# Chunk-band attention beside a gated convolution: taps between the gate's products, end transposes ahead of the second exponential, low parts last in the value products

## The chip, the core and the metric

The kernel runs on one core of one Trainium2 chip. Its engines are TensorE (PE in the profile, with PEld for its weight loads), VectorE (DVE), ScalarE (ACT), GpSimd (POOL) and SyncE (SP, which here only issues DMAs). Each takes its own instructions in the order in which the program gives them, and waits for the others through semaphores. The metric is the device time of one execution in microseconds (us); the kernel before takes 1465.99 us, the median of 3 runs between 1465.03 and 1468.26.

## What is computed

One layer of a streaming encoder, over 2048 prompt frames and 32 frames of a running stream (2080 tokens, width 1024, fp32):

```python
xn = rmsnorm(x, norm_in)
h, bg, cg, zc, q, k, v, za = project_in(xn, w_in)     # 8 x 512 columns
u = cg * h
yc = bg * short_conv(u_ext, conv_w, S) * silu(zc)     # three causal taps along time
ya = band_attention(q, k, v, ...) * silu(za)          # own chunk of 64 and 8 before, 8 heads
x = x + merge_out(yc, ya, norm_conv, norm_att, w_out)
x = per_layer_embed(x, p, ple_norm, w_ple_gate, w_ple_proj)
```

The three taps: `out = w[0] * u_ext[:, 0:length]`, then `out + w[t] * u_ext[:, t:t + length]` for t = 1, 2. The newest keys, values and convolution rows are returned as well.

## The kernel before

Every matrix product is split: a matrix is held as a high part and a low part (what rounding took off), and a product is three products on TensorE, high by high, high by low, low by high. Columns of the projection are worked off in "slots" of 2 x 128 channels, tokens in five chunks of 256, 384, 512, 512 and 416.

The program has four stages. Keys, queries, values and the attention gate come first (to about 400 us of the profiled execution). Then follow the convolution's slots in three passes over the chunks: (0, 1), (2, 3), (4). The first pass runs alone. Beside the second and the third the attention is woven in: `dense()` yields after every three products of `conv` (one contraction slice `k`), and between two yields the main loop takes one "piece" of `attention()` whenever the convolution is ahead of its share. The last stage is the output projection, the embedding gate and the final norm.

`conv(u, banks)` treats one slot. Odd slots are (h, C): they write U = C * h. Even ones are (B, z): block `j == 0` is B, block `j == 1` is z, 24 products each, accumulated in a PSUM bank. Behind the last product of B come the taps: ACT writes T1 (L1097), DVE adds two taps to it (L1099), and DVE multiplies the bank by it (T2, L1102). Behind z come the gate (L1105 to L1107) and the store. All of it is emitted at one place, so on DVE's queue it is one row of instructions.

The attention goes through 68 steps (head pair, 256 queries, head), each with two score blocks `a` of 128 queries by up to 640 keys. One step `n` is six pieces:

- scores of block 0 on PE (L546), and on DVE the bias and the maximum (L558), which reads the scores' two banks; there is only one pair of such banks, so the next scores wait for this maximum
- value products of step n-2 on PE (L650 to L664), and on ACT the exponential of block 0 (L566)
- first transposes of step n-1 (L618), evacuated twice: the high part by ACT (L592), the low part by DVE (L593); then reciprocal (L572, DVE) and normalisation (L578, POOL) of block 0
- scores and maximum of block 1
- second transposes of step n-1, then the exponential of block 1
- the end transposes of step n-1 (L627, L628), then reciprocal and normalisation of block 1

`emit_av` multiplies the values with both parts of the transposed weights (`hi`, `lo`). Middle key tiles go 256 columns at a time (L664); the two end tiles are taken in three products of 64 rows and 128 columns each (L662), ahead of the last middle product.

Of the kernel before, what the change touches and what calls it, by code (L numbers as in the profile page):

```python
# [63 lines left out]
def hybrid_encoder_kernel(  # L64
# [574 lines left out]
    def emit_av(n):  # L639
        p, m, h = steps[n]  # L640
        hi, lo = PT
        p_min = max(0, 4 - 2 * m)
        w = 256 if m < 8 else 2 * S

        heads = [(h, 0)] if m < 8 else [(0, 0), (1, 256 + w)]
        if m == 8:
            for g, _ in heads:
                for k in (1, 2, 3, 0, 4):
                    nk = 256 if k else 128
                    pe.matmul(PS[:, PS_AV, 256 * g:256 * g + nk],  # L650
                              V[:, (16 + k) % RING, g * 128:(g + 1) * 128],
                              hi[:, slot_of[k], 0:nk], start=(k == 1), stop=(k == 4))
        else:
            v = lambda k: V[:, (2 * m - 4 + k) % RING, h * 128:(h + 1) * 128]
            both = [(k, t) for k in range(max(p_min, 1), 5) for t in (hi, lo)]
            for i, (k, t) in enumerate(both):
                if i == len(both) - 1:

                    for k1 in [0, 5] if p_min == 0 else [5]:
                        cs = slice(0, 128) if k1 == 0 else slice(128, 256)  # L660
                        for part, t1 in ((0, hi), (0, lo), (1, hi)):
                            pe.matmul(PS[0:HD, PS_AV, cs], v(k1)[:, part * HD:(part + 1) * HD],  # L662
                                      t1[:, slot_of[k1], cs], start=False, stop=False)
                pe.matmul(PS[:, PS_AV, 0:256], v(k), t[:, slot_of[k], :], start=(i == 0),  # L664
                          stop=(i == len(both) - 1))
        if h == 0:
            ytiles[p, m] = y_r()
        y = ytiles[p, m]
        own = lambda g: slice(64 * g, 64 * g + 64)
        for g, c in heads:  # L670
            act.activation(OFF[own(g), 0:w], PS[own(1 - g), PS_AV, c:c + w], AF.Copy)  # L671
        for g, c in heads:
            dve.tensor_tensor(y[own(g), 0:w], PS[own(g), PS_AV, c:c + w], OFF[own(g), 0:w],
                              ALU.add)
        if h == 1 or m == 8:
            t0, t1 = m * 256, min(m * 256 + 256, TT)
            yt = y[:, 0:t1 - t0]
            if m == 8:
                pool.tensor_tensor(yt, yt, y[:, S:2 * S], ALU.add)
            pool.tensor_tensor(yt, yt, Z[(9 * p + m) % 2][:, 0:t1 - t0], ALU.mult)  # L680
            sp.dma_start(yd[DC + p * 128:DC + (p + 1) * 128, t0:t1], yt)

    def attention():
# [3 lines left out]
        for n in range(N + 2):  # L687
# [24 lines left out]
            if n < N and steps[n][1] == 8:  # L712
                load_bias8(steps[n][0] + 1)
            yield
            if tr:
                tr.pop(0)()
            emit_exp(n, 1)
            yield
            if tr:
                tr.pop(0)()  # L720
            emit_recip(n, 1)
            emit_norm(n, 1)
            if n - 1 in first_of:
# [338 lines left out]
    dve.tensor_scalar(cwh, cT[:, 24:36], 0.5, None, ALU.mult)  # L1062
    dve.memset(carry, 0.0)

    def conv(u, banks):

        kind, cc = slots[NP1 + u % 8][0]
# [8 lines left out]
        for c in chunks:  # L1076
# [3 lines left out]
            for j in range(2):  # L1080
                ps = PS[:, banks(), 0:n]
                js = slice(j * 128, (j + 1) * 128)
                for k in range(KT):
                    for i, (a, b) in enumerate(((wh, Xh), (wh, Xl), (wl, Xh))):
                        pe.matmul(ps, a[:, k, js], b[c][:, k, :], start=(k == i == 0),  # L1085
                                  stop=(k == KT - 1 and i == 2))
                    if k < KT - 1:
                        yield n
                if kind == "h" and j == 0:
                    act.activation(HS[:, :n], ps, AF.Copy)  # L1090
                elif kind == "h":
                    for o, w, x in segs:
                        dve.tensor_tensor(U[:, x:x + w], ps[:, o:o + w], HS[:, o:o + w], ALU.mult)
                elif j == 0:
                    cw = lambda t: cwh[:, 4 * t + cc:4 * t + cc + 1]
                    for o, w, x in segs:
                        act.activation(T1[:, o:o + w], U[:, x - 2:x - 2 + w], AF.Copy, scale=cw(0))  # L1097
                        for t in (1, 2):
                            dve.scalar_tensor_tensor(  # L1099
                                T1[:, o:o + w], U[:, x - 2 + t:x - 2 + t + w], cw(t),  # L1100
                                T1[:, o:o + w], ALU.mult, ALU.add)
                    dve.tensor_tensor(T2[:, :n], ps, T1[:, :n], ALU.mult)  # L1102
                else:

                    act.activation(SZ[:, :n], ps, AF.Tanh, scale=0.5)  # L1105
                    dve.scalar_tensor_tensor(SZ[:, :n], SZ[:, :n], 1.0, ps, ALU.add, ALU.mult)  # L1106
                    pool.tensor_tensor(T2[:, :n], T2[:, :n], SZ[:, :n], ALU.mult)  # L1107
                    sp.dma_start(yd[cc * 128:(cc + 1) * 128, t0:t0 + n], T2[:, :n])
                yield n
# [107 lines left out]
```

## Time and profile before

| | before |
|---|---|
| median of 3 runs | 1465.99 us |
| the profiled execution | 1465.2 us |
| its span, first to last instruction | 1463.2 us |
| granted TensorE clock, mean of the span | 0.992 |
| busy: PE, PEld | 97%, 87% |
| busy: DVE, ACT, POOL | 42%, 37%, 21% |

The profiled execution's own time is 2.0 us longer than its span, and 0.8 us below the median. TensorE is the engine that is nearly always busy. The others have much idle time, and what matters of them is only whether TensorE has to wait for them. A busy share of the whole span hides the stages, so the rows below are read by stretch and as single instructions in order of time.

### The profile page before, as it was taken

What the parts mean: (1) busy time and instruction counts of PE and PEld (TensorE: products, weight loads), DVE (VectorE), ACT (ScalarE), POOL (GpSimd) and SP (SyncE); (2) the same over time, 40 slices, a digit from 0 to 9 for tenths busy, and PEclk for the clock granted to TensorE, in tenths of its full rate; (3) what the DMA queues carried; (4) which work ended last, traced back from release to release, by engine and by line L of the source; (5) the groups of instructions that cost most, each with busy time, mean ns of one, the idle gap of its engine ahead of it and who ended that gap; (6) DMA issues with size and microseconds to landing.
All of it is one profiled execution on the core that took longest, in us unless ns stands there. A gap on an engine that the chain in (4) does not pass through costs nothing.

```text
span 1463.2 us, 22734 instructions
## 1 busy us (share of the span) xinstructions
PE 1426.2 (97%) x8362; PEld 1269.9 (87%) x8362; DVE 609.4 (42%) x1346; ACT 543.5 (37%) x1182; POOL 314.0 (21%) x438
## 2 busy tenths in 40 slices
PE   8999999999999979999999999998999999999997
PEld 8889989999899968888888888997788888888786
DVE  6323233330044326656555566653424333242333
ACT  7434233341233125544544544552122232232323
POOL 3310000000000013323332232331223232233322
PEclk9999999999999999999999999999999999999999
DMA  6536898884277555453555347666932212121100
GB/s 222 196 109 198 294 314 312 292 286 149 79 249 260 213 183 180 159 163 122 170 174 195 126 148 270 251 231 232 363 102 69 72 48 93 48 80 40 60 25 33
DMA packets 176391, 249.10 MB, mean 170 GB/s; under 512 B 19564, under 2 KB 124816, under 8 KB 170136
## 3 DMA queue, kind: packets, MB, share of 16 engines
q1 hardware_dynamic: 169712, 235.83, 47.6%
q10 hardware_dynamic: 6568, 11.82, 2.5%
q8 instruction: 66, 1.08, 0.3%
q14 instruction: 45, 0.37, 0.1%
HBM read 158.23 MB, written 92.50 MB: 171 GB/s over the span
## 4 chain that ended last, share of the span: by engine, by line
PE 86%; DMA 5%; DVE 3%; issue 2%; ACT 2%; SPq 1%; POOL 1%; POOLq 0%; DVEq 0%; ACTq 0%
PE PS L1085 20%; PE PS L279 17%; PE PS L280 16%; PE PS L281 16%; PE PS L546 5%; PE PS L664 3%; PE PS L618 3%; DMA GR<-wd 2%; PE PS L662 1%; PE PS L871 1%; DMA GR<-qs 1%; PE PS L829 1%; PE PS L268 1%; DMA GF<-ext 1%; DVE GF L1099 1%
## 5 line engine op out<-in xcount | busy, mean ns | idle before, releaser
L279 PE MATMUL PS<-GR 128*128 128x512 f32 (+3 forms) x1336 | 476.2, 356 | 2.9 <-DVE GF L1120 1.8
L280 PE MATMUL PS<-GR 128*128 128x512 f32 (+3 forms) x1336 | 471.9, 353 | 1.1 <-DVE GR L271 0.6
L281 PE MATMUL PS<-GR 128*128 128x512 f32 (+3 forms) x1336 | 471.9, 353 | 0.5 <-DVE GR L812 0.5
L1085 PE MATMUL PS<-GR 128*128 128x512 f32 (+3 forms) x1920 | 432.1, 361 | 0.6 <-DMA GR<-wc 0.6
L1085 PEld LDWEIGHTS PS<-GR 128*128 128x128 f32 x1920 | 310.8, 191 | 16.8 <-DMA GR<-wc 0.9
L279 PEld LDWEIGHTS PS<-GR 128*128 128x128 f32 x1336 | 253.2, 190 | 34.2 <-DVE GF L1120 2.1
L281 PEld LDWEIGHTS PS<-GR 128*128 128x128 f32 x1336 | 253.1, 189 | 31.6 <-DVE GR L812 1.0
L280 PEld LDWEIGHTS PS<-GR 128*128 128x128 f32 x1336 | 253.4, 190 | 30.9 <-DMA GR<-wd 1.1
L578 POOL TENSOR_SCALAR GF<-GF,SM 128x640 f32<-128x640 f32 (+3 forms) x132 | 98.5, 746 | 265.7 <-DVE SM L572 195.8
L593 DVE TENSOR_TENSOR GR<-PS,GR 128x256 fp32r<-128x256 f32 (+2 forms) x184 | 103.2, 562 | 98.9 <-ACT GR L592 98.7
L592 ACT ACTIVATE GR<-PS 128x256 fp32r<-128x256 f32 (+2 forms) x184 | 89.8, 489 | 78.4 <-PE PS L618 76.7
L1107 POOL TENSOR_TENSOR GF<-GF 128x512 f32<-128x512 f32 (+3 forms) x20 | 22.4, 1122 | 409.1 <-DVE GF L1106 408.4
L566 ACT ACTIVATE GF<-GF,SM 128x640 f32<-128x640 f32 (+3 forms) x132 | 99.9, 757 | 22.7 <-DVE SM L558 21.4
L558 DVE CUSTOM_DVE_ANT_0 GF<-PS,GF 128x640 f32<-128x640 f32 (+3 forms) x132 | 96.2, 729 | 24.7 <-PE PS L546 20.8
L546 PE MATMUL PS<-GR 128*128 128x320 f32 (+6 forms) x512 | 94.9, 307 | 11.7 <-DMA GR<-qs 7.4
L546 PEld LDWEIGHTS PS<-GR 128*128 128x128 f32 x512 | 81.4, 190 | 20.9 <-issue 7.7
L910 DVE TENSOR_TENSOR GF<-PS,GF 128x512 f32<-128x512 f32 (+2 forms) x35 | 23.6, 675 | 176.3 <-ACT GF L909 176.3
L909 ACT ACTIVATE GF<-PS,SM 128x512 f32<-128x512 f32 (+2 forms) x35 | 23.6, 675 | 163.9 <-PE PS L281 82.7
L664 PE MATMUL PS<-GR 128*128 128x256 f32 x448 | 78.0, 289 | 3.0 <-DVE GR L593 3.0
L195 DVE SCALAR_TENSOR_TENSOR GR<-GF,cT,GR 128x256 fp32r<-128x256 f32 x112 | 45.8, 480 | 73.9 <-ACT GR L194 73.9
L912 POOL TENSOR_TENSOR GF<-GF 128x512 f32<-128x512 f32 (+1 forms) x32 | 41.1, 1285 | 159.7 <-DVE GF L910 141.5
L671 ACT ACTIVATE GF<-PS 64x256 f32<-64x256 f32 (+1 forms) x72 | 26.0, 360 | 130.7 <-PE PS L664 124.2
(139 smaller groups left out, 1344.4 us busy)
## 6 DMA issues: line engine op xcount, KB each, us to landing
GR<-wc SPq DMA_DIRECT2D x32, 1024.0 KB, 7.3
GR<-wd SPq DMA_DIRECT2D x72, 256.0 KB, 6.8
GF<-in_x_prompt_dram SPq DMA_DIRECT2D x32, 512.0 KB, 7.6
wc<-GR SPq DMA_DIRECT2D x16, 1024.0 KB, 7.6
GR<-qs SPq DMA_DIRECT2D x128, 128.0 KB, 3.2
wd<-GF SPq DMA_DIRECT2D x50, 256.0 KB, 6.1
GF<-in_w_in_dram SPq DMA_DIRECT2D x20, 512.0 KB, 6.0
vd<-GF SPq DMA_DIRECT2D x40, 256.0 KB, 5.1
```

Of the source, the lines that this page charges most:

```text
L195: dve.scalar_tensor_tensor(wl[:, k], RAW[:, k], cT[:, k:k + 1], wh[:, k].bitcast(F32), ALU.mult, ALU.subtract)
L279: pe.matmul(out, wh(k), xh(k), start=(k == ks_[0]), stop=False)
L280: pe.matmul(out, wh(k), xl(k), start=False, stop=False)
L281: pe.matmul(out, wl(k), xh(k), start=False, stop=(k == ks_[-1]))
L546: pe.matmul(ps[:, e, c:c + n_], q[h][b][:, qa], K[h][:, r:r + n_], start=(b == 0 and c == 0), stop=(b == 1), skip_group_check=True)
L558: dve.tensor_tensor_reduce(pr.rearrange("p (b c) -> p b c", b=nb), ps, br.rearrange("p (b c) -> p b c", b=nb), 1.0, 3e38, ALU.add, ALU.min ...
L566: act.activation(pr, pr, AF.Exp, bias=mx[rows], scale=-1.0, accum_out=sm[rows])
L578: pool.tensor_scalar(pr, pr, rs[rows], 1.0, ALU.mult, ALU.mult)
L592: act.activation(dst_of(hi), src, AF.Copy)
L593: dve.tensor_tensor(dst_of(lo), src, dst_of(hi).bitcast(F32), ALU.subtract)
L664: pe.matmul(PS[:, PS_AV, 0:256], v(k), t[:, slot_of[k], :], start=(i == 0), stop=(i == len(both) - 1))
L1085: pe.matmul(ps, a[:, k, js], b[c][:, k, :], start=(k == i == 0), stop=(k == KT - 1 and i == 2))
```

## The change

Three pieces of code move, and none is added or taken away.

The taps of `conv` go out of the place behind B's last product. A new function `tap` emits tap 0 (ACT) after the products of slice k = 1 of the block B, tap 1 after k = 3 and tap 2 after k = 5 (both DVE). Only the product T2 stays behind the last product. In `attention` the end transposes and their evacuation move from the sixth piece into the fifth, ahead of the second exponential. In `emit_av` the high parts of all middle tiles are multiplied first and then the low parts, and the ends go high, high, low.

```diff
-            both = [(k, t) for k in range(max(p_min, 1), 5) for t in (hi, lo)]
+            both = [(k, t) for t in (hi, lo) for k in range(max(p_min, 1), 5)]
...
-                        for part, t1 in ((0, hi), (0, lo), (1, hi)):
+                        for part, t1 in ((0, hi), (1, hi), (0, lo)):
...
             yield
-            if tr:
+            while tr:
                 tr.pop(0)()
             emit_exp(n, 1)
             yield
-            if tr:
-                tr.pop(0)()
             emit_recip(n, 1)
             emit_norm(n, 1)
...
+    TAP_AT = (1, 3, 5)
+
+    def tap(t, cc, segs):
+        cw = cwh[:, 4 * t + cc:4 * t + cc + 1]
+        for o, w, x in segs:
+            src = U[:, x - 2 + t:x - 2 + t + w]
+            if t == 0:
+                act.activation(T1[:, o:o + w], src, AF.Copy, scale=cw)
+            else:
+                dve.scalar_tensor_tensor(T1[:, o:o + w], src, cw, T1[:, o:o + w],
+                                         ALU.mult, ALU.add)
...
+                    if kind == "B" and j == 0 and k in TAP_AT:
+                        tap(TAP_AT.index(k), cc, segs)
                     if k < KT - 1:
                         yield n
...
                 elif j == 0:
-                    cw = lambda t: cwh[:, 4 * t + cc:4 * t + cc + 1]
-                    for o, w, x in segs:
-                        act.activation(T1[:, o:o + w], U[:, x - 2:x - 2 + w], AF.Copy, scale=cw(0))
-                        for t in (1, 2):
-                            dve.scalar_tensor_tensor(
-                                T1[:, o:o + w], U[:, x - 2 + t:x - 2 + t + w], cw(t),
-                                T1[:, o:o + w], ALU.mult, ALU.add)
                     dve.tensor_tensor(T2[:, :n], ps, T1[:, :n], ALU.mult)
```

VectorE's queue at the B block of the second pass whose taps run at 657 us of the profiled execution, before (L558 is a maximum, L593 a low part, L572 a reciprocal, L673 the sum of the two value halves):

```order
L558 ISA GF,SM<-PS,GF 128x384
L558 ISA SM 128x1
L673 TENSOR_TENSOR GF<-PS,GF 64x256
L572 RECIPROCAL SM<-SM 128x1
L558 ISA GF,SM<-PS,GF 128x512
L558 ISA SM 128x1
L593 TENSOR_TENSOR GR<-PS,GR 128x256
L1099 SCALAR_TENSOR_TENSOR GF<-GF,cwh 128x512 x2
L1102 TENSOR_TENSOR GF<-PS,GF 128x512
L593 TENSOR_TENSOR GR<-PS,GR 128x128
L572 RECIPROCAL SM<-SM 128x1
```

The same place now (L1073 is a tap, L1108 is T2):

```order
L1073 SCALAR_TENSOR_TENSOR GF<-GF,cwh 128x512
L558 ISA GF,SM<-PS,GF 128x384
L558 ISA SM 128x1
L673 TENSOR_TENSOR GF<-PS,GF 64x256
L1073 SCALAR_TENSOR_TENSOR GF<-GF,cwh 128x512
L572 RECIPROCAL SM<-SM 128x1
L558 ISA GF,SM<-PS,GF 128x512
L558 ISA SM 128x1
L593 TENSOR_TENSOR GR<-PS,GR 128x256
L593 TENSOR_TENSOR GR<-PS,GR 128x128
L1108 TENSOR_TENSOR GF<-PS,GF 128x512
L572 RECIPROCAL SM<-SM 128x1
```

The two taps left the place between the two low parts for places in front of a maximum and in front of a reciprocal, the second low part (the ends') stands directly behind the first, and T2 stands behind both.

The same queue at the B block whose taps run at 587 us, before:

```order
L673 TENSOR_TENSOR GF<-PS,GF 64x256
L593 TENSOR_TENSOR GR<-PS,GR 128x512
L572 RECIPROCAL SM<-SM 128x1
L1099 SCALAR_TENSOR_TENSOR GF<-GF,cwh 128x512 x2
L1102 TENSOR_TENSOR GF<-PS,GF 128x512
L558 ISA GF,SM<-PS,GF 128x640
L558 ISA SM 128x1
L593 TENSOR_TENSOR GR<-PS,GR 128x512
```

And now:

```order
L1073 SCALAR_TENSOR_TENSOR GF<-GF,cwh 128x512
L673 TENSOR_TENSOR GF<-PS,GF 64x256
L593 TENSOR_TENSOR GR<-PS,GR 128x512
L572 RECIPROCAL SM<-SM 128x1
L1108 TENSOR_TENSOR GF<-PS,GF 128x512
L558 ISA GF,SM<-PS,GF 128x640
L558 ISA SM 128x1
L593 TENSOR_TENSOR GR<-PS,GR 128x512
```

In front of the maximum only T2 is left; one tap stands ahead of L673, and the other one a maximum further up.

ScalarE's queue in a step of the second pass without a tap, before (L566 is an exponential, L592 a high part; the last one is that of the ends):

```order
L671 ACTIVATE GF<-PS 64x256
L566 ACTIVATE GF,SM<-GF,SM 128x640
L592 ACTIVATE GR<-PS 128x512 x2
L566 ACTIVATE GF,SM<-GF,SM 128x640
L592 ACTIVATE GR<-PS 128x2x128
```

And now:

```order
L671 ACTIVATE GF<-PS 64x256
L566 ACTIVATE GF,SM<-GF,SM 128x640
L592 ACTIVATE GR<-PS 128x512 x2
L592 ACTIVATE GR<-PS 128x2x128
L566 ACTIVATE GF,SM<-GF,SM 128x640
```

The ends' high part went ahead of the second exponential.

## Rows read from the trace of the kernel before

**Rows 1.** The page's line of busy time, share of the span and instructions of each engine.

```profile
PE 1426.2 (97%) x8362; PEld 1269.9 (87%) x8362; DVE 609.4 (42%) x1346; ACT 543.5 (37%) x1182; POOL 314.0 (21%) x438
```

**Rows 2.** Busy time by stretch: the first pass of the convolution, and the second and third with the attention beside them. Columns: stretch, its length, busy time and instructions of PE, PEld, DVE, ACT and POOL, granted clock of PE, DMA share, GB/s.

```profile
400.00:520.00 120.00, 120.00 (x802) 118.75 (x801) 43.54 (x104) 35.13 (x83) 8.33 (x12) 1.00 0.65 230
520.00:1016.00 496.00, 475.32 (x3076) 425.20 (x3075) 278.89 (x744) 231.55 (x565) 140.86 (x215) 0.99 0.56 187
```

**Rows 3.** The waits view of PE between 580 and 1010 us: who waited, for whom, total us, times, longest.

```profile
PE PS L546 <- DVE SM L558: 4.3, 4, 1.7
PE PS L662 <- DVE GR L593: 4.2, 2, 2.2
PE PS L664 <- DVE GR L593: 3.0, 3, 1.3
PE PS L618 <- POOL GF L578: 0.8, 3, 0.3
```

**Rows 4.** The timeline around the taps at 657 us: start, duration, engine, line, operation, tiles, count, and in brackets the idle time before and what ended it.

```profile
657.10 0.25 ACT L592 ACTIVATE GR<-PS 128x128 fp32r<-128x128 f32 x1
657.23 1.54 DVE L1099 SCALAR_TENSOR_TENSOR GF<-GF,cwh 128x512 f32<-128x512 f32 x2 [1.16 <-ACT GF L1097]
657.61 0.22 PE L662 MATMUL PS<-GR 128*64 128x128 f32 x1
658.86 0.69 DVE L1102 TENSOR_TENSOR GF<-PS,GF 128x512 f32<-128x512 f32 x1
659.47 0.28 DVE L593 TENSOR_TENSOR GR<-PS,GR 128x128 fp32r<-128x128 f32 x1
659.80 0.34 PE L662 MATMUL PS<-GR 128*64 128x128 f32 x2 [1.97 <-DVE GR L593]
```

**Rows 5.** The timeline around the taps at 587 us, same columns.

```profile
587.15 1.94 DVE L1099 SCALAR_TENSOR_TENSOR GF<-GF,cwh 128x512 f32<-128x512 f32 x2
587.43 1.12 POOL L578 TENSOR_SCALAR GF<-GF,SM 128x640 f32<-128x640 f32 x1 [1.13 <-DVE SM L572]
589.29 0.69 DVE L1102 TENSOR_TENSOR GF<-PS,GF 128x512 f32<-128x512 f32 x1 [0.20 <-DVE GF L1099]
589.89 0.81 DVE L558 CUSTOM_DVE_ANT_0 GF<-PS,GF 128x640 f32<-128x640 f32 x1
590.77 0.41 PE L546 MATMUL PS<-GR 128*128 128x320 f32 x1 [1.72 <-DVE SM L558]
```

**Rows 6.** Busy time by stretch, columns as in Rows 2: two short stretches behind the waits at 657 and 774 us, and the three long ones around them.

```profile
661.70:665.10 3.40, 3.40 (x12) 2.72 (x11) 1.19 (x4) 0.28 (x2) 0.89 (x2) 0.50 0.50 161
777.80:781.10 3.30, 3.30 (x11) 2.52 (x10) 0.92 (x3) 1.33 (x4) 1.53 (x3) 0.50 0.14 43
581.70:661.60 79.90, 75.88 (x498) 66.28 (x497) 45.14 (x122) 38.48 (x97) 22.80 (x40) 1.00 0.50 164
665.20:777.70 112.50, 108.94 (x711) 95.10 (x711) 67.84 (x176) 55.75 (x137) 34.07 (x53) 1.00 0.47 152
781.20:1016.00 234.80, 229.52 (x1538) 212.21 (x1537) 133.63 (x353) 109.52 (x263) 66.42 (x98) 1.00 0.62 213
```

**Rows 7.** The taps on DVE between 530 and 1010 us: count, shortest, median and longest duration in ns, first and last start, forms; they belong to 11 B blocks.

```profile
L1099 DVE SCALAR_TENSOR_TENSOR GF<-GF,cwh x28: 239/750/1168, 562.7 to 989.5; 128x512 f32<-128x512 f32 x16, 128x384 f32<-128x384 f32 x6, 128x32 f32<-128x32 f32 x6
```

**Rows 8.** From the groups by line and form between 520 and 1010 us: count, busy us, mean ns of one, idle before.

```profile
L1099 DVE SCALAR_TENSOR_TENSOR GF<-GF,cwh 128x512 f32<-128x512 f32 x16 | 13.3, 832 | 2.3 <-ACT GF L1097 2.1
L1102 DVE TENSOR_TENSOR GF<-PS,GF 128x512 f32<-128x512 f32 x8 | 5.5, 691 | 1.2 <-DVE GF L1099 0.6 <-PE PS L618 0.2
```

**Rows 9.** The timeline of a step without a tap: a maximum, its read-out, and the scores behind it; then the second exponential's read-out, the ends' high part and low part, and the reciprocal.

```profile
603.43 0.82 DVE L558 CUSTOM_DVE_ANT_0 GF<-PS,GF 128x640 f32<-128x640 f32 x1
604.17 0.08 DVE L558 DVE_READ_ACCUMULATOR2_ANT SM<- 128x1 f32 x1
604.31 0.95 PE L546 MATMUL PS<-GR 128*128 128x320 f32 x6
...
605.03 0.18 ACT L566 ACTIVATION_READ_ACCUMULATOR GF<-GF,SM 128x1 f32 x1
605.12 0.36 ACT L592 ACTIVATE GR<-PS 128x256 fp32r<-128x256 f32 x1
605.51 0.42 DVE L593 TENSOR_TENSOR GR<-PS,GR 128x256 fp32r<-128x256 f32 x1 [0.50 <-ACT GR L592]
605.85 0.15 DVE L572 RECIPROCAL SM<-SM 128x1 f32<-128x1 f32 x1
```

**Rows 10.** The timeline around 884 us: a product on POOL, a copy of two columns on DVE, and the scores that waited.

```profile
883.86 1.29 POOL L1107 TENSOR_TENSOR GF<-GF 128x512 f32<-128x512 f32 x1 [0.64 <-DVE SM L572]
883.90 1.28 DVE L1075 COPY GF<-cT 128x2 f32<-128x2 f32 x1
885.57 0.61 PE L546 MATMUL PS<-GR 128*128 128x384 f32 x2 [0.47 <-DVE SM L558]
```

**Rows 11.** The timeline at the end of the first pass, and the first scores of the attention.

```profile
516.46 0.56 DVE L1102 TENSOR_TENSOR GF<-PS,GF 128x384 f32<-128x384 f32 x1 [9.39 <-DMA yd<-GF]
527.97 0.75 PE L546 MATMUL PS<-GR 128*128 128x128 f32 x2 [7.35 <-DMA GR<-qs]
```

**Rows 12.** The timeline of the last B block, where the last stage begins.

```profile
1016.00 1.06 ACT L811 ACTIVATE GR<-GR 128x1024 fp32r<-128x1024 f32 x1 [13.62 <-DMA GR<-yd]
1023.00 0.50 PE L279 MATMUL PS<-GR 128*128 128x512 f32 x1 [1.85 <-DVE GF L1120]
```

## The prediction

> **What bounds the kernel now.** I read the page's busy shares first, then busy time by stretch, then the waits of TensorE, then single instructions around each wait, and last the granted clock behind them. TensorE is busy 97% of the span and every other engine under half [rows 1], so an instruction on another engine costs time only where TensorE waits for it. The stretches show where that can be: in the convolution's first pass, 400 to 520 us, TensorE is busy 120.00 of 120.00 us, and there the taps hold up nothing that counts; in the second and third pass, with the attention beside them, it is busy 475.32 of 496.00 us, which leaves 20.7 us idle [rows 2]. Of these 7.35 us are one wait at 528 us for queries [rows 11]. The rest is mostly in the waits view from 580 to 1010 us: 4.3 us of scores (L546) waiting for a maximum (L558), 4.2 and 3.0 us of value products (L662, L664) waiting for a low part (L593), 0.8 us of transposes waiting for POOL [rows 3].
>
> The single instructions show what these have in common. At 657 us the ends' high part is done at 657.35, and its low part, 0.28 us long, could start. But VectorE's queue holds the two taps (1.54 us) and T2 (0.69 us) in front of it; the low part runs at 659.47, and TensorE has waited 1.97 us for it [rows 4]. At 587 us the same three instructions stand in front of a maximum. It runs at 589.89 instead of about 587.2, and the next scores wait 1.72 us [rows 5]. The reader is to see a queue taken in order: 2.2 to 2.6 us of work that nobody waits for, ahead of 0.3 to 0.9 us for which TensorE waits. I followed the nine rows of waits of rows 3 on DVE to their places: eight stand behind such a bunch; the ninth, 0.47 us, stands behind a copy [rows 10].
>
> **The taps.** The change removes no instruction. 11 B blocks lie in the attention's stretch, with 28 tap instructions on DVE [rows 7], in 22 places (the third pass cuts a tap in two). Before, each block's pair and its T2 were one bunch: 2 x 0.83 + 0.69 = 2.35 us by the means [rows 8]. Now the largest piece is one tap, 0.83 us, or T2. Of the waits this takes away those behind a bunch: 4.3 - 0.47 + 4.2 + 3.0 = 11.0 us [rows 3, 10].
>
> A second term hangs on the first. Behind the waits of about 2 us at 657 and 774 us the granted clock is 0.50, that is 1.2 in place of 2.4 GHz, for 3.4 and 3.3 us; the long stretches around them have 1.00, though the shorter waits lie in them, that of 1.72 us among them [rows 5, 6]. Work done at half the clock takes twice the time, so half of 6.7 us was lost: 3.35 us. Without the two waits I expect no fall there.
>
> Against this stands what a single tap costs at its new place. It is put between the products, and so in front of whatever DVE does there: a maximum, a low part, a reciprocal. The trace does not show a tap there, so I bound it. From below: nothing, since DVE is busy only 278.89 of 496.00 us there [rows 2], and an idle stretch hides a tap. Less than nothing I exclude for this part, since the order of the other instructions is kept. From above: all of it on TensorE at all places, 13.3 us for the 16 long ones [rows 8] and 6 x 0.75 = 4.5 us for the third pass by the median [rows 7], 17.8 us. What decides is the room between a maximum and the scores behind it. It can be thin: in one step the read-out ends at 604.25 and the scores start at 604.31 [rows 9]. But a whole bunch of 2.35 us cost TensorE 11.0 / 8 = 1.4 us on average at eight of the 11 blocks and nothing at three, so that about 1 us and more was covered each time, and a single tap is mostly covered. I take the lower end and add three waits of the size of the thin case at 885.57, 0.47 us each [rows 10]: 1.4 us given back.
>
> Tap 0 moves on ScalarE from behind B to slice 1, where it needs U. In the third pass U is written right before, so ScalarE may stand behind DVE for part of a microsecond, three times, with an exponential behind it. I put this into the 1.4 us. The first pass and the last B block keep their waits. At 516 us T2 waits for the store of the previous T2, and the queries come after that store [rows 11]; neither depends on the taps. At 1016 us the last block's taps stand on ScalarE behind an instruction that waits 13.62 us for a transfer [rows 12], and they still stand behind it.
>
> **The end transposes.** Two transposes a step go one piece earlier on TensorE, which costs it nothing, since the normalised weights that they read are the ones that the first transposes have read already. On ScalarE the second exponential now starts one high part later, 0.36 us. On DVE the reciprocal still comes behind the ends' low part, but that one no longer comes behind the exponential: before, the reciprocal started at 605.85, 0.64 us behind the read-out at 605.21 [rows 9]; now the read-out would end 0.36 us later, at 605.57, and the reciprocal could follow directly. So POOL's normalisation starts some 0.2 us earlier, not later. Bounds: all of TensorE's waits for POOL gone, 0.8 us [rows 3], or three of them longer by 0.36 us, 1.1 us. I take zero. What the move also does is to bring the ends' low part ahead of T2, which helps at 657 us even if the taps alone did not.
>
> **The value products.** Here the wait for a low part moves back by one to three products, of which each is a small part of the waits of 2 us. It works on the same 7.2 us as the taps and can't win them a second time. As cover for the thin cases it is inside the 1.4 us.
>
> **The sum.** 11.0 + 3.35 - 1.4 = 13.0 us. The profiled execution took 1465.2 us, 2.0 us more than its span and 0.8 us less than the median, so 1465.2 - 13.0 + 0.8 gives 1453.0 us.
>
> **The rivals.** First, the waits go, but the clock falls elsewhere as often as before, since other gaps stay: 1465.2 - 11.0 + 1.4 + 0.8 = 1456.4 us. For it speaks that the wait of 7.35 us stays; against it, that from 781 to 1016 us, with two of the three waits on L664 and the one of rows 10 in it, the clock held 1.00 [rows 6].
>
> Second, the taps meet POOL. A copy of two columns took 1.28 us beside a product on POOL of 1.29 us, from start to end [rows 10]. POOL is busy 140.86 of 496.00 us there [rows 2], 28%, so some 6 of 22 taps would meet it; if each held DVE for 1.13 us more where it has no room, 6.8 us would come back: 1459.8 us. Against it speaks that the tap pair beside POOL took 1.94 us [rows 5] where the one without took 1.54 us [rows 4]: 0.4 us more, not 1.1. The Trainium skill, "SBUF — State Buffer", section "Who interferes with whom", holds that VectorE and GpSimd share one pair of ports and that it is an exclusive lock, behind which the loser waits for the whole instruction. The trace agrees for the copy and not for the taps; by the rule taken literally the forecast would be this rival's.
>
> Third, the change does not do what it says: the maximum was late for another reason than the bunch, and the waits come back at other steps. Then the time stays within 0.2% of before, about what a measurement of this kernel can tell from no change, 1466 us. Against it stands that nothing else was in front of the late instructions [rows 4, 5].
>
> Fourth, slower: every single tap lands in front of a maximum whose scores have no room, as at 604.31 [rows 9]. Then 17.8 us come in for the 14.35 us that go, 1465.2 + 3.4 + 0.8 = 1469.4 us. It decides from the point where four in five taps (14.35 of 17.8) are without cover; DVE's idle 44% speaks against that.
>
> **How the numbers follow.** Chances: the forecast 0.62, the first rival 0.15, the second 0.13, the third 0.05, the fourth 0.05. The forecast's own range goes from 1448.5 us (nothing given back, POOL's 0.8 us won, and some 2 us that the modelled ends of the matmuls hide) to 1457 us. The first rival lies inside. About half of the second does if the range ends at 1459 us. That holds 0.62 + 0.15 + 0.06 = 0.83. Faster by over 0.2% (under 1463.1 us): 0.62 + 0.15 + 0.13 = 0.90; same 0.05; slower 0.05.
>
> **What would show it.** In the waits of TensorE between 580 and 1010 us, no row on L593's successor, and 1.5 us or less behind the maximum: the taps' term. Granted clock 1.00 in every stretch from 581 to 1010 us: the clock's term; a 0.50 there with the waits gone speaks for the first rival. Taps of 1.2 us and more beside POOL, with scores waiting behind them, for the second. Waits for POOL's normalisation above 0.8 us would show the end transposes mis-sized. The waits at 528 and 1023 us should stand as they are. The forecast is wrong if maxima wait behind single taps at many steps.

## The result and the profile after

The changed kernel takes 1450.59 us (median of 6 runs, 1448.02 to 1454.36), the one before 1465.51 us (6 runs, 1462.56 to 1468.26). The ratio is 0.990, with a 95% interval of 0.988 to 0.992: about 15 us, or 1.0%, faster. The prediction was 1453.0 us, in a range of 1448.5 to 1459.0 us.

The profiled execution of the kernel after took 1452.0 us with a span of 1450.1 us, 13.1 us shorter than the span before. The page's line of busy time shows the same work as [rows 1]:

```profile
PE 1421.2 (98%) x8362; PEld 1270.3 (88%) x8362; DVE 607.8 (42%) x1346; ACT 542.3 (37%) x1182; POOL 317.4 (22%) x438
```

Busy time by stretch (columns as in [rows 2]): the first pass, the one short stretch at half clock beside the attention, and the rest of the attention's stretch:

```profile
400.00:520.00 120.00, 120.00 (x803) 118.86 (x802) 43.62 (x104) 34.63 (x83) 8.33 (x12) 1.00 0.65 229
524.30:534.60 10.30, 6.24 (x17) 5.12 (x18) 0.89 (x5) 1.10 (x4) 0.37 (x1) 0.50 0.92 311
534.60:1003.00 468.40, 464.52 (x3062) 421.06 (x3060) 276.77 (x740) 230.14 (x562) 142.84 (x214) 1.00 0.56 189
```

The first pass is as it was. To compare the attention's stretch one has to cut both traces at the same work. These two windows hold the same 3078 products of TensorE, up to the first product of the output projection (L279); the first is the kernel before, the second the kernel after:

```profile
520.00:1017.11 497.11, 475.86 (x3078) 425.33 (x3076) 278.90 (x745) 232.66 (x567) 140.86 (x215) 0.99 0.56 187
520.50:1002.56 482.06, 470.94 (x3078) 426.07 (x3077) 277.23 (x745) 231.37 (x567) 143.21 (x215) 0.99 0.57 192
```

So the attention's stretch is 15.05 us shorter, 2 us more than the span. Of that, 0.5 us was lost ahead of 520.50 us and 1.5 us behind 1002.56 us, where TensorE waits 1.8 us for the last stage's weights (1.12, 0.17 and 0.50 us) and the kernel before 0.5 us. Inside the stretch TensorE's idle time went from 497.11 - 475.86 = 21.25 to 482.06 - 470.94 = 11.12 us, which is 10.1 us. The other 4.9 us are busy time, of which the granted clock explains about half, as worked out below.

The waits of TensorE between 520 and 995 us show what went (columns as in [rows 3]; the row of the queries answers to the 7.35 us in [rows 11]):

```profile
PE PS L546 <- DMA GR<-qs: 7.2, 1, 7.2
PE PS L618 <- POOL GF L578: 2.0, 3, 0.7
PE PS L546 <- DVE SM L558: 0.5, 1, 0.5
PE PS L1096 <- DMA GR<-wc: 0.4, 1, 0.4
```

The 7.2 us for low parts are gone, and of the 4.3 us for maxima 0.5 us is left, the wait behind the copy of [rows 10]. POOL's row grew. The timeline at the place of [rows 4], now at 655 us, shows the cause at work:

```profile
654.73 0.56 ACT L592 ACTIVATE GR<-PS 128x256 fp32r<-128x256 f32 x2 [1.08 <-PE PS L618]
...
655.18 0.62 DVE L593 TENSOR_TENSOR GR<-PS,GR 128x256 fp32r<-128x256 f32 x2
...
655.72 0.68 DVE L1108 TENSOR_TENSOR GF<-PS,GF 128x512 f32<-128x512 f32 x1
...
657.14 0.34 PE L662 MATMUL PS<-GR 128*64 128x128 f32 x3
```

Both low parts come straight behind their high parts, and T2 (L1108) stands behind them. The product L662, which had waited 1.97 us, has no bracket: it waits for nothing.

### The profile page after: what moved, and what is told of

Same layout as the page of the kernel before. It is cut to its first block, busy times and chain, and to the rows that moved or that the text cites. A ratio compares the mean times of both kernels' runs of the same rounds, so it can differ in the third digit from the quotient of the medians.

```text
span 1450.1 us, 22728 instructions
## 1 busy us (share of the span) xinstructions
PE 1421.2 (98%) x8362; PEld 1270.3 (88%) x8362; DVE 607.8 (42%) x1346; ACT 542.3 (37%) x1182; POOL 317.4 (22%) x438
## 4 chain that ended last, share of the span: by engine, by line
PE 90%; DMA 4%; issue 2%; DVE 2%; ACT 1%; POOL 1%; SPq 1%; POOLq 0%; ACTq 0%; DVEq 0%
PE PS L1096 22%; PE PS L279 17%; PE PS L280 17%; PE PS L281 17%; PE PS L546 5%; PE PS L664 4%; PE PS L618 3%; PE PS L662 1%; PE PS L869 1%; PE PS L827 1%; PE PS L268 1%; DMA GR<-wd 1%; DMA GF<-ext 1%; DVE GR L209 1%; DMA GR<-qs 0%
## 5 line engine op out<-in xcount | busy, mean ns | idle before, releaser
L279 PE MATMUL PS<-GR 128*128 128x512 f32 (+3 forms) x1336 | 476.4, 357 | 4.2 <-DVE GF L1126 1.7
L279 PEld LDWEIGHTS PS<-GR 128*128 128x128 f32 x1336 | 253.4, 190 | 35.6 <-DVE GF L1126 1.9
L578 POOL TENSOR_SCALAR GF<-GF,SM 128x640 f32<-128x640 f32 (+3 forms) x132 | 99.7, 756 | 243.7 <-DVE SM L572 178.3
L593 DVE TENSOR_TENSOR GR<-PS,GR 128x256 fp32r<-128x256 f32 (+2 forms) x184 | 97.6, 559 | 73.3 <-ACT GR L592 72.9
L1113 POOL TENSOR_TENSOR GF<-GF 128x512 f32<-128x512 f32 (+3 forms) x20 | 22.4, 1121 | 411.4 <-DVE GF L1112 400.6
L592 ACT ACTIVATE GR<-PS 128x256 fp32r<-128x256 f32 (+2 forms) x184 | 83.7, 491 | 75.5 <-PE PS L618 74.8
L558 DVE CUSTOM_DVE_ANT_0 GF<-PS,GF 128x640 f32<-128x640 f32 (+3 forms) x132 | 96.9, 734 | 28.4 <-PE PS L546 24.6
L566 ACT ACTIVATE GF<-GF,SM 128x640 f32<-128x640 f32 (+3 forms) x132 | 100.4, 761 | 16.6 <-DVE SM L558 15.8
```

The lines of the kernel that those rows point to most:

```text
L279: pe.matmul(out, wh(k), xh(k), start=(k == ks_[0]), stop=False)
L558: dve.tensor_tensor_reduce(pr.rearrange("p (b c) -> p b c", b=nb), ps, br.rearrange("p (b c) -> p b c", b=nb), 1.0, 3e38, ALU.add, ALU.min ...
L566: act.activation(pr, pr, AF.Exp, bias=mx[rows], scale=-1.0, accum_out=sm[rows])
L578: pool.tensor_scalar(pr, pr, rs[rows], 1.0, ALU.mult, ALU.mult)
L592: act.activation(dst_of(hi), src, AF.Copy)
L593: dve.tensor_tensor(dst_of(lo), src, dst_of(hi).bitcast(F32), ALU.subtract)
```

## The experiments

Each was timed in five rounds against the kernel before; ratios carry their 95% intervals. Kernels of one job shared a chip and the runs of before: e1 to e4 (before 1465.59 us), e5 to e8 (1466.27), e9 to e11 (1466.14), e12 (1466.09). The theory was that of the prediction: a bunch on DVE's queue is in front of short work for which TensorE waits. The rivals were that one of the other two parts does it (e2, e3), that the place of the taps counts and not the bunch's length (e4), and that single taps cost something that was not seen (e7).

One correction for the expectations: they put the waits for POOL's normalisation at 2.7 us after and 1.3 us before. In the 2.7 us the wait at about 579 us was counted in two windows that both show it, and the 1.3 us add two rounded rows. The row above gives 2.0 us in three waits; before it was 1.2 us in four.

**e1: the taps alone**, in the kernel before.

```diff
+                    if kind == "B" and j == 0 and k in TAP_AT:
+                        tap(TAP_AT.index(k), cc, segs)
...
-                    for o, w, x in segs:
-                        act.activation(T1[:, o:o + w], U[:, x - 2:x - 2 + w], AF.Copy, scale=cw(0))
-                        for t in (1, 2):
...
```

> The kernel before with the taps alone moved between the products of B. Theory (the bunch of two taps and T2 on VectorE's queue is what TensorE waited for): nearly the whole gain, 10 to 14 us under before, ratio 0.990 to 0.993, and in TensorE's waits between 580 and 1010 us less than 1.5 us behind L558 and L593 together, where before had 11.5 us. Rival (the gain comes from the end transposes and the order of the value products): 0 to 4 us under before, ratio 0.997 to 1.000, with the waits on the low part (L593, 7.2 us before) still there.

1449.69 us, 0.9902 [0.9889, 0.9915]: the whole gain. The waits of TensorE in e1, 520 to 995 us:

```profile
PE PS L546 <- DMA GR<-qs: 8.3, 1, 8.3
PE PS L618 <- POOL GF L578: 0.9, 3, 0.5
PE PS L546 <- DVE SM L558: 0.5, 1, 0.5
PE PS L1098 <- DMA GR<-wc: 0.2, 1, 0.2
PE PS L662 <- DVE GR L593: 0.2, 1, 0.2
```

The same 11 us went, without the two other parts, and POOL's row did not grow.

**e2: the end transposes alone.**

```diff
-            if tr:
+            while tr:
                 tr.pop(0)()
             emit_exp(n, 1)
             yield
-            if tr:
-                tr.pop(0)()
```

> The kernel before with the end transposes alone moved ahead of the second exponential. Theory: at the two longest waits (657 and 774 us, 4.2 us together) only the ends' low part stood behind the bunch, and now it stands ahead of it, so these two go, with 1.7 us of half clock behind each; the waits of the scores behind the maximum (3.8 us) and the other value products (3.0 us) stay: 4 to 8 us under before, ratio 0.9945 to 0.9975. Rival (the second exponential starts 0.36 us later and the normalisation on POOL with it): no gain or up to 2 us slower, with TensorE's waits for L578 above 2 us, where before had 1.3 us.

1463.85 us, 0.9989 [0.998, 0.9999]: 1.7 us, far less than the 4 to 8 us expected and than the 4.2 us of waits on L662 that it should end. The waits between 580 and 1010 us, and the timeline at the place of [rows 4]:

```profile
PE PS L618 <- POOL GF L578: 5.9, 4, 2.3
PE PS L546 <- DVE SM L558: 4.3, 4, 1.7
PE PS L664 <- DVE GR L593: 3.0, 3, 1.3
```

```profile
656.62 1.54 DVE L1097 SCALAR_TENSOR_TENSOR GF<-GF,cwh 128x512 f32<-128x512 f32 x2 [0.97 <-ACT GF L1095]
...
658.25 0.69 DVE L1100 TENSOR_TENSOR GF<-PS,GF 128x512 f32<-128x512 f32 x1
...
658.86 0.15 DVE L572 RECIPROCAL SM<-SM 128x1 f32<-128x1 f32 x1
...
659.21 0.69 POOL L578 TENSOR_SCALAR GF<-GF,SM 128x512 f32<-128x512 f32 x1 [4.75 <-DMA GR<-qs]
...
659.95 0.33 PE L618 MATMUL PS<-ident,GF 128*128 128x128 f32 x1 [2.34 <-POOL GF L578]
```

The low part is out of the bunch's way, and the waits on L662 are gone. But now the reciprocal (0.15 us) is the next short work behind the bunch, POOL's normalisation behind that, and TensorE waits 2.34 us where it had waited 1.97. (The bracket at L578 names a transfer; by order of time the reciprocal is what it needed.) The wait moved, since the bunch was still there: POOL's row took 5.1 us (5.9 for 0.8) where 4.2 us went. So it is not less waiting that made e2 faster; its profile lacks the fall of the clock at 777 us (last section), which cost 1.7 us before.

**e3: the order of the value products alone.**

```diff
-            both = [(k, t) for k in range(max(p_min, 1), 5) for t in (hi, lo)]
+            both = [(k, t) for t in (hi, lo) for k in range(max(p_min, 1), 5)]
...
-                        for part, t1 in ((0, hi), (0, lo), (1, hi)):
+                        for part, t1 in ((0, hi), (1, hi), (0, lo)):
```

> The kernel before with the order of the value products alone changed (high parts first). Theory: the wait for a low part moves back by one to three products, 0.1 to 0.3 us at each of five waits: 0.5 to 1.5 us under before, which can't be told from no change, ratio 0.998 to 1.001; the waits on L593 stay at 5 us or more of 7.2. Rival (the order alone covers the low part): the waits on L593 under 2 us, 5 to 9 us under before, ratio 0.994 to 0.9965.

1465.08 us, 1.0001 [0.9993, 1.001]: no change. The waits for low parts are 4.1 and 2.6 us, where [rows 3] have 4.2 and 3.0.

**e4: the taps as one bunch at the first place**, slice 1, in the changed kernel; T2 stays behind the last product.

```diff
-    TAP_AT = (1, 3, 5)
+    TAP_AT = (1, 1, 1)
...
-                        tap(TAP_AT.index(k), cc, segs)
+                        for t in range(3):
+                            tap(t, cc, segs)
```

> The changed kernel, but with all three taps together after slice 1 of B: the bunch is kept, without T2, at another place. Theory (length of the bunch decides): two taps are 1.66 us in one piece where the kernel before had 2.35 us, so some waits come back: 3 to 8 us over the changed kernel, ratio to before 0.992 to 0.9965, with 2 to 6 us of waits of TensorE behind L558 and L593. Rival (what hurt was the place behind B's last product, not the bunch): as fast as the changed kernel within 2 us, ratio 0.989 to 0.9915, waits behind L558 and L593 under 1 us.

1456.46 us, 0.9949 [0.9937, 0.9961]: slower than e1 on the same chip by 6.8 us and than the kernel after by 5.9 us, with intervals apart. The waits between 580 and 1000 us, and one place of them:

```profile
PE PS L618 <- POOL GF L578: 3.2, 4, 1.2
PE PS L546 <- DVE SM L558: 1.8, 3, 0.8
PE PS L527 <- DVE SM L558: 0.7, 1, 0.7
```

```profile
579.66 2.40 DVE L1073 SCALAR_TENSOR_TENSOR GF<-GF,cwh 128x512 f32<-128x512 f32 x2
...
580.29 1.24 POOL L578 TENSOR_SCALAR GF<-GF,SM 128x640 f32<-128x640 f32 x1
581.58 0.20 PEld L618 LDWEIGHTS PS<-ident,GF 128*128 128x128 f32 x2 [1.41 <-POOL GF L578]
581.58 0.44 PE L618 MATMUL PS<-ident,GF 128*128 128x128 f32 x2 [1.17 <-POOL GF L578]
```

So the earlier place is not what helps; two taps in a row cost there too. No row on L593 came back, but from 520 to 1000 us the maxima's waits are 2.5 us where the kernel after has 0.5, and POOL's row is 4.3 us where it has 2.0. The place shown is a second way in which a pair costs: beside the normalisation it took 2.40 us instead of 1.54, and the normalisation 1.24 us instead of 0.80.

**e5: the attention starts later**: 6.5% of the two passes' products before its first piece, in place of 3%. The aim was the wait for the queries, and with it the fall of the clock at 524 us.

```diff
-    FIRST, END = 0.03, 0.94
+    FIRST, END = 0.065, 0.94
```

> The changed kernel with the attention's start put off from 3% to 6.5% of the convolution's second and third pass, some 9 us of products later, so that the queries are there when the first scores want them. Theory (the granted clock falls behind waits of TensorE of 2 us and more, and what falls is lost): the wait of 7.2 us at 521 us goes, and so does the half clock behind it, 10.2 us at 0.50 in the changed kernel, which is 5.1 us lost: 10 to 13 us under the changed kernel, ratio to before 0.981 to 0.984. Rival (the clock falls at its own times, whatever waits): only the wait goes, 6 to 8 us under the changed kernel, ratio 0.984 to 0.987, with a stretch at 0.50 of 7 to 10 us still between 515 and 545 us.

1447.50 us, 0.9876 [0.9852, 0.9900]: some 3 us under the kernel after by the medians, with intervals that overlap, and not 10 to 13. Two stretches of e5, and a wait:

```profile
515.00:545.00 30.00, 30.00 (x147) 24.99 (x147) 10.39 (x36) 9.32 (x25) 4.67 (x8) 1.00 0.73 250
870.10:876.80 6.70, 5.63 (x20) 5.21 (x21) 1.84 (x6) 1.96 (x6) 0.58 (x1) 0.50 0.57 183
```

```profile
871.17 0.55 PE L664 MATMUL PS<-GR 128*128 128x256 f32 x1 [4.09 <-DMA GR<-vd]
```

At 524 us both are gone. But 350 us later the values' transfer, issued at 862.91 us right behind the loads of the next pass's weights, comes 4.09 us late, and the clock falls during that wait instead, at 869.99 us.

**e6: the gate's last product on DVE** instead of POOL, in the changed kernel.

```diff
-                    pool.tensor_tensor(T2[:, :n], T2[:, :n], SZ[:, :n], ALU.mult)
+                    dve.tensor_tensor(T2[:, :n], T2[:, :n], SZ[:, :n], ALU.mult)
```

> The changed kernel with the gate's last product (T2 times SZ) on VectorE instead of GpSimd. Theory (what is left of TensorE's waits beside the attention, 2.7 us behind the normalisation, is the same queueing on GpSimd: a product of 1.28 us stands ahead of a normalisation of 0.80 us): the waits for L578 between 520 and 1010 us fall under 1 us, 1 to 3 us under the changed kernel, ratio to before 0.988 to 0.990. Rival (the normalisation is late because the exponential is): the waits for L578 stay above 2 us, and VectorE's added 0.7 us brings new waits behind maxima, 0 to 3 us over the changed kernel.

1448.24 us, 0.9878 [0.9858, 0.9897]: 2.4 us under the kernel after by the medians, with intervals that overlap. The waits for POOL, 520 to 995 us, fell from 2.0 to 0.9 us; a new one of 0.7 us came up at the end transposes:

```profile
PE PS L546 <- DMA GR<-qs: 7.0, 1, 7.0
PE PS L618 <- POOL GF L578: 0.9, 3, 0.4
PE PS L627 <- DVE GR L593: 0.7, 1, 0.7
```

What the gate's product does on POOL's queue is seen in the timeline of the kernel after, at the first of its three waits for POOL:

```profile
577.39 0.15 DVE L572 RECIPROCAL SM<-SM 128x1 f32<-128x1 f32 x1
...
577.56 1.28 POOL L1113 TENSOR_TENSOR GF<-GF 128x512 f32<-128x512 f32 x1 [2.27 <-DVE SM L572]
578.82 0.80 POOL L578 TENSOR_SCALAR GF<-GF,SM 128x640 f32<-128x640 f32 x1
579.67 0.44 PE L618 MATMUL PS<-ident,GF 128*128 128x128 f32 x2 [0.73 <-POOL GF L578]
```

The reciprocal is done at 577.54 us, and the normalisation begins at 578.82, behind the gate's product of 1.28 us (L1113). The two other waits, at 691.78 and 852.24 us, stand behind the same pair.

**e7: no DVE taps** in the changed kernel. It leaves out taps 1 and 2.

```diff
-            else:
-                dve.scalar_tensor_tensor(T1[:, o:o + w], src, cw, T1[:, o:o + w],
-                                         ALU.mult, ALU.add)
```

> The changed kernel with the two taps on VectorE left out (tap 0 alone stays, so the convolution's output lacks two of its three terms). It measures what the single taps still cost at their new places. Theory (a single tap is nearly always covered; the prediction gave back 1.4 us): 0 to 2 us under the changed kernel, ratio to before 0.988 to 0.9905. Rival (single taps still cost a good part of the bunch): 4 us or more under the changed kernel, ratio under 0.987.

1451.88 us, 0.9905 [0.9883, 0.9926]: no different from the kernel after, as far as intervals of 3 us to either side can tell. Its waits say more: the same 2.0 us for POOL and 0.5 us for the maximum. At their new places 28 taps cost TensorE no wait.

**e8: the taps alone, with the gate on DVE and the start of e5.** The edits are those of e1, e6 and e5.

```diff
...
-                    pool.tensor_tensor(T2[:, :n], T2[:, :n], SZ[:, :n], ALU.mult)
+                    dve.tensor_tensor(T2[:, :n], T2[:, :n], SZ[:, :n], ALU.mult)
...
-    FIRST, END = 0.03, 0.94
+    FIRST, END = 0.065, 0.94
```

> The kernel before with the taps alone moved, the attention's start put off to 6.5%, and the gate's last product on VectorE. If the three are independent: 13 to 18 us under the kernel with the taps alone moved, of which the start is 10 to 13 and the gate 1 to 3, ratio to before 0.978 to 0.982. If the clock falls at its own times: 7 to 11 us under it, ratio 0.983 to 0.9855.

1445.85 us, 0.9864 [0.9843, 0.9886]: some 4 us under e1, not 13 to 18. TensorE waits 3.9 us in seven waits for maxima, and 2.3 us for the values' transfer that is late in e5.

**e9, e10, e11: e8 with the start at 0.05, at 0.08, and at the old 0.03** (so e11 is e1 with the gate on DVE).

```diff
-    FIRST, END = 0.03, 0.94
+    FIRST, END = 0.05, 0.94
```

```diff
-    FIRST, END = 0.03, 0.94
+    FIRST, END = 0.08, 0.94
```

```diff
-                    pool.tensor_tensor(T2[:, :n], T2[:, :n], SZ[:, :n], ALU.mult)
+                    dve.tensor_tensor(T2[:, :n], T2[:, :n], SZ[:, :n], ALU.mult)
```

> The taps alone moved, the gate's last product on VectorE, the attention's start at 5% of the convolution: the first scores stand behind 57 products of the second pass, not 33, that is some 5.5 us later, and should wait about 2 us for the queries, where they waited 7 to 8. Theory (half clock comes behind waits of about 2 us and more): a fall may or may not follow this wait, none where nothing waits over 2 us; ratio to before 0.982 to 0.987. Rival (falls come at their own times): two or three stretches at 0.50 anywhere, ratio 0.986 to 0.990.

> The same with the start at 8%: the first scores stand behind 87 products, some 12 us later than at 3%, and wait for nothing. The other waits, for values at the change of head pair, depend on where the weights' loads fall and are not foreseen. Theory: no fall between 515 and 545 us; if no transfer is late, a granted clock of 0.997 or more and a ratio to before of 0.981 to 0.985; if one is late by over 2 us, a fall right behind it and 0.985 to 0.988. Rival: a fall with no wait of 1.5 us or more in the 15 us ahead of it.

> The taps alone moved and the gate's last product on VectorE, the start at 3% as in the changed kernel: the end transposes and the value products as before. Theory (these two parts bring nothing): within 2 us of the changed kernel with the gate on VectorE (1448.24 us), ratio to before 0.987 to 0.990. Rival (the end transposes bring something that the taps' move hid): 3 us or more over it, ratio above 0.990, with waits behind L593 of 2 us or more.

e9 1445.61 us, 0.9859 [0.9836, 0.9883]; e10 1446.58 us, 0.9869 [0.9846, 0.9892]; e11 1449.75 us, 0.9882 [0.9863, 0.9902]. In e9 the queries cost 2.5 us in two waits and the low parts 2.5 us in four, no transfer of values is late, and the clock is full from 515 to 1000 us. e10 waits 2.4 us for queries at 640 us, without a fall of the clock, and 2.0 us for values at 874 us, with one. e11 stands to e6 as the kernel without the two small parts to the one with them: waits of 1.5 us for low parts (L662) and 0.2 us for POOL against none and 0.9, and two times that can't be told apart.

**e12: the changed kernel with the gate on DVE and the start at 0.05.**

```diff
-                    pool.tensor_tensor(T2[:, :n], T2[:, :n], SZ[:, :n], ALU.mult)
+                    dve.tensor_tensor(T2[:, :n], T2[:, :n], SZ[:, :n], ALU.mult)
...
-    FIRST, END = 0.03, 0.94
+    FIRST, END = 0.05, 0.94
```

> The changed kernel whole (taps, end transposes, value products), with the gate's last product on VectorE and the start at 5%. Against the same with the taps alone (1445.61 us, ratio 0.9859), where TensorE waited 2.5 us for the ends' low part (L662 behind L593). Theory (with the bunch gone, the end transposes trade a wait for the low part against one for the normalisation): the waits of L662 behind L593 under 0.5 us, in their place 1 to 2.5 us behind L578 or a wait of the next transposes behind L593; within 2 us of it, ratio 0.9845 to 0.9875. Rival (the end transposes are worth having once the rest is out of the way): 2.5 us or more under it, ratio under 0.984, with the waits for L578 and L593 together under 1 us.

1444.85 us, 0.9856 [0.984, 0.9873]: the lowest time here, some 6 us or 0.4% under the kernel after by medians of different jobs, with ratios to before whose intervals do not meet. It is within 1 us of e9. The waits between 515 and 990 us are 3.0 us for queries in three waits, 1.4 us for POOL and 1.1 us for maxima.

## Why the prediction was right, step by step

**The taps' 11.0 us** was right in mechanism and size. The eight waits behind the bunch are gone and the ninth, behind the copy, stands. e1 shows that the taps' part alone does it, e2 and e3 that the others don't, and e4 that two taps in a row cost again at another place, some 6 of the 15 us. Tap 0 went along on ScalarE, and no run moves it alone; that VectorE's queue is what made TensorE wait rests on [rows 4] and [rows 5], where the late instructions stand behind the bunch.

**The clock's 3.35 us** was right in kind. The two falls at 661 and 777 us are gone; from 534.6 to 1003 us the clock is 1.00. In this pair of executions the term came to less, since the fall at the wait for the queries is longer after. In the kernel before, TensorE did 4.03 us of work at half the clock there:

```profile
525.20:532.00 6.80, 4.03 (x10) 3.31 (x11) 0.46 (x3) 0.50 (x2) 0.37 (x1) 0.50 0.95 321
```

After it is 6.24 us, so (6.24 - 4.03) / 2 = 1.1 us came back, and the term is 3.35 - 1.1 = 2.25 us. The change did not do that: this fall is 10.2 us long in the kernel after, in e1 and e4, and also in e3 with the taps of before; it is 6.8 us long before and in e2, and also in e6, e7 and e11 with the taps moved. Nor has every execution of the old queue both of the falls that the term was read from: e3 waits 1.91 us at 657 us without one (last section). So one profile was a narrow base for the term. More executions bear it out: the granted clock was 0.9916 on average in 44 further executions of the kernel before and 0.9937 in the six of the kernel after. As an estimate, span times what is missing to 1, that is 12.3 and 9.2 us, 3.2 us apart.

**The busy time** that is gone is 4.9 us, and 2.25 us of it is the clock. Some 2.7 us are left over. The prediction had "some 2 us that the modelled ends of the matmuls hide" in the lower end of its range and not in its sum. Whether these are short stalls is not shown; it stays open.

**The 1.4 us given back** was put on the single taps, as three waits like that of 0.47 us. e7 shows that they cost no wait. What did come back has another source, the end transposes.

**The end transposes, taken as zero**, is the step that was wrong. They cost 1.1 us, the upper one of the step's two bounds, and its own sign for that came, waits for POOL above 0.8 us. TensorE waits for the normalisation at three places. Before these waits are 0.47, 0.21 and 0.21 us (578, 696 and 862 us), after 0.73, 0.73 and 0.55 us (580, 692 and 852 us). e1 has the values of before, and e2, which moves the end transposes alone, those of after, both to 0.01 us. (The row grew by 0.8 us only, 1.2 to 2.0, because a fourth wait of 0.33 us behind the bunch went with the taps.)

The step followed the reciprocal, and that was on time. It left out the gate. The gate's tanh (L1111, in e1 L1113) stands on ScalarE's queue right behind the second exponential (L566), which now comes behind the ends' high part; the gate's product on POOL needs it, and the normalisation stands behind that product. The place at 579 us in e1:

```profile
575.53 0.82 ACT L566 ACTIVATE GF<-GF,SM 128x640 f32<-128x640 f32 x1
576.34 0.59 ACT L1113 ACTIVATE GF<-PS 128x512 f32<-128x512 f32 x1
...
577.73 1.29 POOL L1115 TENSOR_TENSOR GF<-GF 128x512 f32<-128x512 f32 x1 [2.01 <-DVE GF L1114]
577.90 0.15 DVE L572 RECIPROCAL SM<-SM 128x1 f32<-128x1 f32 x1
...
579.01 0.79 POOL L578 TENSOR_SCALAR GF<-GF,SM 128x640 f32<-128x640 f32 x1
...
579.86 0.44 PE L618 MATMUL PS<-ident,GF 128*128 128x128 f32 x2 [0.47 <-POOL GF L578]
```

And in the kernel after, ahead of the rows shown under e6:

```profile
575.34 0.83 ACT L566 ACTIVATE GF<-GF,SM 128x640 f32<-128x640 f32 x1
576.16 0.59 ACT L1111 ACTIVATE GF<-PS 128x512 f32<-128x512 f32 x1
```

Counted from the start of the span all of this is earlier in the kernel after, but so is TensorE: it is ready for the transposes at 579.67 - 0.73 = 578.94 us, in e1 at 579.86 - 0.47 = 579.39 us. Counted back from there, the exponential begins 3.60 us ahead after and 3.86 us in e1, the tanh 2.78 and 3.05, the gate's product 1.38 and 1.66, the normalisation 0.12 and 0.38. Each is 0.26 to 0.28 us later, and so the wait is 0.26 us longer. The reciprocal ends 1.40 and 1.34 us ahead: 0.06 us earlier, as the step had it, and without effect. At the two other places the same four start 0.5 and 0.3 us later. e6 took the gate's product off POOL, and the row fell to 0.9 us.

The prediction also said that the move "helps at 657 us even if the taps alone did not"; e2 shows that the wait there only goes over to the normalisation.

**The value products at nothing**: right (e3). **The waits that should stand**, those for the queries (7.35 to 7.24 us) and at the start of the last stage (1.85 to 1.7 us), do.

**The sum** was 13.0 us, and the two spans differ by 13.1 us. That they agree so closely is luck. The attention's stretch, of which the sum speaks, won 15.05 us: 10.1 us of idle time (11.0 us less 0.8 us of POOL's row and 0.1 us of smaller gaps), 2.25 us of clock and the 2.7 us in busy time. In this one execution 2.0 us were lost outside it. In e1 they were not, and its span is 15.4 us shorter than before; the medians of before and after differ by 14.9 us. So the sum was some 2 us short of what the change brings, and what it lacked is the busy time that stays open. The spread of single runs follows the clock (the six executions of after: mean granted clock 0.995 with a span of 1446.1 us to 0.991 with 1452.5). The lower end of the range comes to 1448.8 us by its own terms, not 1448.5.

**The rivals.** The clock did not fall at other places of the attention's stretch, against the first. The time speaks against the third and the fourth, and e7 against the fourth's taps. The second, that taps meet POOL, is right in kind and small in cost: in the kernel after, the 16 long taps took 764 ns on average where [rows 8] have 832, and e7 finds no cost. The Trainium skill, "SBUF — State Buffer", section "Who interferes with whom", says that a VectorE instruction with two SBUF inputs contends with a GpSimd instruction that reads SBUF. The tap reads U and T1, and the trace agrees. It agrees with the exclusive lock that the prediction cites, too, and the prediction misread its own rows there: one has to look at the ends and not at the durations. In [rows 5] the pair of taps ends at 589.09 us, 0.54 us behind the normalisation (588.55); in e4 it ends at 582.06 us, 0.53 us behind it (581.53). In the fourteen traces 70 taps of 128x512 began while a normalisation had over 0.2 us to run, and 66 of them ended 0.53 or 0.54 us behind its end. (The other four, all at 855 to 859 us, ran their plain 0.74 us, and the normalisation ended 0.59 us behind them.) A tap alone takes 0.73 us, so being held costs it what the normalisation still has to run less 0.2 us, and that is why the rival's 1.13 us for each was too much.

## What to carry to other kernels

When an engine with much idle time still delays the engine that bounds the kernel, look at what stands in its queue ahead of the late instruction: here 2.35 us of work that nobody waited for cost 11 us in eight places, and pieces of 0.8 us between other work cost no wait (e7). Making the late instruction earlier instead only hands the wait to the next short instruction behind the same bunch (e2). And of a step that is moved, follow every queue down to the engine that is waited for: the reciprocal was on time, but the exponential that came 0.26 to 0.5 us later had the gate's tanh behind it, and through it POOL's queue was late.

## What the runs showed of the hardware beyond that

Between 515 and 1030 us the fourteen traces have 24 falls of the granted clock to 0.50. 22 of them begin during a wait of TensorE of 1.8 us or more, or less than 2 us behind one; the two others, after at 1019.3 us and e4 at 1025.4 us, begin 2.7 us behind a wait of 1.12 us and during one of 1.48 us. Where a wait was taken away its fall went too (the two behind the bunch; in e5 the one at 524 us), and where e5 got a new wait, for the values, it got a new fall. But not every such wait has a fall: of 29 waits of 1.8 us or more, seven between 1.84 and 2.38 us have none (one in e2, two each in e3 and e10, one each in e6 and e11). In e2 the wait of 2.34 us at 657 us has one, and that of 2.30 us, which ended at 777.34 us, has none. In e3, with the queue of before, the wait of 1.91 us, which ended at 659.65 us, has none. Two stretches of e2 and one of e3:

```profile
660.60:664.00 3.40, 3.40 (x12) 2.71 (x11) 1.19 (x4) 0.10 (x1) 0.74 (x2) 0.50 0.54 169
775.00:782.00 7.00, 4.70 (x26) 4.01 (x26) 4.62 (x14) 2.56 (x7) 2.15 (x4) 1.00 0.30 86
650.00:670.00 20.00, 17.69 (x101) 14.86 (x100) 11.88 (x35) 9.28 (x26) 5.17 (x9) 1.00 0.69 231
```

So what a wait of about 2 us costs is its length and, in some cases, half of 3.4 us of work on top. Which it will be could not be told from these traces; that stays open.
